# A fused decoder step: the first projected tile by feature blocks, a norm moved, a lane turn more, and sums of squares in two passes

## The chip, the cores and the metric

The kernel runs on one core of a Trainium2 chip. The core has a matrix engine (TensorE, PE in the profile; its weight loads are listed apart as PEld), a vector engine (DVE), a scalar engine (ACT), GpSimd (POOL) and a queue engine (SP) that issues most transfers. The metric is device microseconds of one execution, the median over the runs; lower is better.

## The reference, cut to what matters

Two layers of a hybrid decoder run on 512 prompt tokens and 32 sample tokens that share every weight. Inputs are scaled so that the attention weights are sharp, and all is float32. What the change touches:

```
hn = rmsnorm(x, norm_g);  z = hn @ w_in            # 10080 columns, 79 tiles of 128
k  = rmsnorm((rmsnorm(mem, g) @ w_k) by head, gk)  # memory keys, 256 rows
c  = rmsnorm(kv_lat, kv_norm_g)                    # kv_lat: 128 columns of z
qf = rmsnorm(q_lat, q_norm_g) @ w_uq               # q_lat: 192 columns of z
y_hg = rmsnorm(o_hg by head, hg_g)                 # after the HGRN recurrence
x  = x + merged @ w_out
```

`rmsnorm` divides a row by the root of the mean of its squares. The rest (short convolution, HGRN2 recurrence, attention over latents in pages and over memory keys, gated branch outputs) is in the kernel but is not edited.

## The kernel before

Everything is kept with features on the 128 partitions and the 544 tokens along the free axis, so a sum over features is a matrix product with a matrix of ones. A large product takes a weight block of 128 x 1024 at a time (an item): the scalar engine copies it to a type float32r (`wh`, the high part), the vector engine subtracts that from the float32 block (`wl`, the low part), and TensorE adds three products per feature block and half of the tokens (272 columns): high x high, high x low, low x high, in float32r. The activations are split the same way (`Hh`, `Hl` of the normed x). An item of `w_in` is 48 such products. A `wh`/`wl` pair of buffers exists twice, so the pair of the next item but one waits until an item has been multiplied.

The main loop goes over 254 items per execution: 8 of memory keys and values (`mk`, `mv`), then per layer the projected tiles C (the latent of keys), B and A (query latent and rope), `mq` (memory query), the others, and at the end 8 of `w_out`. Between the two halves of an item it takes a turn of lane `a` (memory attention, HGRN recurrence), after an item a turn of lane `b` (latent attention); a turn runs to the next `yield`. Items 30 to 99 of a layer give lane `b` no turn at every fourth item. The names `ta`, `tb` (`ra`, `rb` when float32r) are the lanes' buffers of 128 x 544, `sm` and `big` are accumulators, `sl` and `s` are two pools of six small tiles each. The framework puts the instructions of all engines in order by a built-in timeline, so an edit can shift instructions far from it; each engine then runs its own list strictly in that order.

What the prediction's steps touch, by name in the code: `xn_finish` (inverse norm of x, its broadcast by TensorE as `sm<-cst,sl`, then per block `e`, `Hh`, `Hl`); `ev_memk`, which sums the squares of the memory keys, normalizes and multiplies by the gain `kgb`, and `memk_T`, eight transposes of those keys at L514; `z_mm`, the products of an item; `rstd_big`, which turns sums into inverse roots by ACT (copy with epsilon, a table load, logarithm, a table load, exponential, square) and two DVE steps; and in `lane_b` the norm of C, then the norm of the query latent (tiles A and B), then `q_mm` for four heads, whose first product reads the normed `qA`. The sums of squares of C, of the query latent and of the four HGRN heads multiply by `ones`, a float32 matrix.

Of the kernel before, what the change touches and what calls it, by code (L numbers as in the profile page):

```python
# [19 lines left out]
P = 128  # L20
# [5 lines left out]
KD = 8  # L26
# [109 lines left out]
def hybrid_kernel(ctx: ExitStack, tc: tile.TileContext, a, o):  # L136
# [32 lines left out]
    def mm(out, lhsT, rhs, start=True, stop=True):  # L169
        return TE.matmul(out, lhsT, rhs, start=start, stop=stop)  # L170

    def act(out, in_, f, **k):
        S.activation(out, in_, f, **k)  # L173
# [54 lines left out]

    ident = cs_("id", P)
    ones = kp.tile([P, P], F32, name="ones")  # L230
    epsc = kp.tile([P, 1], F32, name="epsc")
    row4 = kp.tile([P, 4, P], F32R, name="row4")
    csq = kp.tile([P, T], F32, name="csq")

    def setup_first():
        V.memset(ones, 1.0)
        V.memset(epsc, EPS)
        x = t("b")[:, 0:4 * P].rearrange("p (h q) -> p h q", h=4)
        G.memset(x, 0.0)
        for h in range(4):  # L240
            G.memset(x[32 * h:32 * h + 1, h, :], 1.0)
        V.tensor_copy(row4, x)
        G.memset(cnew, 0.0)
        S.dma_start(out=gn, in_=a["gains"])
# [37 lines left out]
    def rstd_big(srcs, n, rows=P):  # L282

        v, y, z = t(), t(), t()
        w = 0
        for ap in srcs:
            k = ap.shape[-1]
            act(v[:rows, w:w + k], ap, AF.Identity, scale=1.0 / n, bias=epsc[:rows])
            w += k
        v, yv, z = v[:rows, :w], y[:rows, :w], z[:rows, :w]  # L290
        act(yv, v, AF.Ln)
        act(yv, yv, AF.Exp, scale=-0.5)
        act(z, yv, AF.Square)
        stt(z, z, -0.5, v, ALU.mult, ALU.mult)
        stt(yv, z, 1.5, yv, ALU.add, ALU.mult)
        return y

    def rstd_small(ss, n, alloc=None, eng=None):

        rows, w = ss.shape  # L300
        alloc = alloc or s_
        v, y, z = (x[:rows, :w] for x in (alloc(), alloc(), alloc()))
        ts(v, ss, 1.0 / n, EPS, ALU.mult, ALU.add)
        ts(y.bitcast(I32), v.bitcast(I32), -0.5, float(0x5F3759DF), ALU.mult, ALU.add)
        for _ in range(3):
            if eng is None:
                tt(z, y, y, ALU.mult)
                stt(z, z, -0.5, v, ALU.mult, ALU.mult)
                stt(y, z, 1.5, y, ALU.add, ALU.mult)
            else:  # L310
                tt(z, y, y, ALU.mult, eng=eng)
                tt(z, z, v, ALU.mult, eng=eng)
                ts(z, z, -0.5, 1.5, ALU.mult, ALU.add, eng=eng)
                tt(y, y, z, ALU.mult, eng=eng)
        return y
# [38 lines left out]
    def z_mm(l, key):  # L354
        def run(it, half):
            if half == 0:
                it.ps = big()
            Hh, Hl = st[l]["H"]
            for k in range(KD):
                w = slice(k * P, (k + 1) * P)  # L360
                c = slice(half * HT, (half + 1) * HT)
                for n, (x, y) in enumerate(((it.hi, Hh), (it.hi, Hl), (it.lo, Hh))):
                    mm(it.ps[:, half, 0:HT], x[:, w], y[:, k, c], start=(k == 0 and n == 0), stop=(k == KD - 1 and n == 2))
        return run

    def proj_mm(l):
# [41 lines left out]
    def ps2(it):  # L408
        return it.ps[:, :, 0:HT]
# [76 lines left out]

    def ev_memk(l):
        def run(it):
            ss = s_()
            kr = []  # L490
            for mt in range(2):
                x, q = t(), t("b")
                act(x[:, 0:512], it.ps[:, mt, :], AF.Copy, scale=rmem[:, mt:mt + 1])
                act(q[:, 0:512], it.ps[:, mt, :], AF.Square, scale=rmem[:, mt:mt + 1])
                red(ss[:, 4 * mt:4 * mt + 4], q[:, 0:512].rearrange("p (h d) -> p h d", h=4), ALU.add)
                kr.append(x)
            r = rstd_small(ss[:, 0:8], P)
            for mt in range(2):
                kv = kr[mt][:, 0:512].rearrange("p (h d) -> p h d", h=4)
                tt(kv, kv, bc(r[:, 4 * mt:4 * mt + 4], P), ALU.mult)  # L500
                tt(kv, kv, bcl(kgb[:, l, :], 4), ALU.mult)
                defer(2, lambda mt=mt: SY.dma_start(out=o["mk"][l, :, mt, :], in_=kr[mt][:, 0:512]))
            st[l]["kr"] = kr
        return run

    def memk_T(l):
# [23 lines left out]
    def ev_C(l):  # L530
        def run(it):
            lane[0] = "b"
            st[l]["kvr"], st[l]["sqkv"] = t(), t()
            act(v2(st[l]["kvr"]), ps2(it), AF.Copy)
            act(v2(st[l]["sqkv"]), ps2(it), AF.Square)
        return run

    def ev_B(l):
# [16 lines left out]
    def ev_A(l):  # L555
        def run(it):
            lane[0] = "b"
            qA, sqA = t(), t()
            act(v2(qA), ps2(it), AF.Copy)
            act(v2(sqA), ps2(it), AF.Square)  # L560
            st[l].update(qA=qA, sqA=sqA)
        return run

    def ev_mq(l, h):
# [272 lines left out]
    def hgrn(l, h):  # L837
# [190 lines left out]
        act(ob[:, 0:TP], ps, AF.Copy)  # L1028
        act(ob[:, TP:T], pso[:, 0:32], AF.Copy)
        act(sq, ob, AF.Square)  # L1030
        yield
        srcs = [sm(), sm()]
        for hf in range(2):
            mm(srcs[hf][:, 0:HT], ones, sq[:, hf * HT:(hf + 1) * HT])
        r = rstd_big([p[:, 0:HT] for p in srcs], P)
        stt(ob, ob, g_("hgn", 4 * l + h), r, ALU.mult, ALU.mult)
        st[l]["yh", h] = ob
        yield
# [2 lines left out]
    def lane_b(l):  # L1041
# [6 lines left out]
        SY.dma_start(out=wuqA[:, 0:512], in_=a["wuq"][l, 0:P])  # L1048
        G.memset(wuqB[64:128, 0:512], 0.0)
        SY.dma_start(out=wuqB[0:64, 0:512], in_=a["wuq"][l, P:192])  # L1050
        kvr, sqkv, qA, qB, sqA, sqB, rt, r2 = (st[l].pop(k) for k in ("kvr", "sqkv", "qA", "qB", "sqA", "sqB", "rt", "r2"))
        srcs = [sm(), sm()]
        for hf in range(2):
            mm(srcs[hf][:, 0:HT], ones, sqkv[:, hf * HT:(hf + 1) * HT])
        r = rstd_big([p[:, 0:HT] for p in srcs], P)
        cT = kvr
        stt(cT, kvr, g_("kv", l), r, ALU.mult, ALU.mult)
        defer(2, lambda: SY.dma_start(out=o["c"][l], in_=cT))
        yield
        srcs = [sm(), sm()]  # L1060
        for hf in range(2):
            c = slice(hf * HT, (hf + 1) * HT)
            mm(srcs[hf][:, 0:HT], ones, sqA[:, c], stop=False)
            mm(srcs[hf][:, 0:HT], ones, sqB[:, c], start=False)
        r = rstd_big([p[:, 0:HT] for p in srcs], 192)
        stt(qA, qA, g_("qa", l), r, ALU.mult, ALU.mult)
        stt(qB[0:64], qB[0:64], g_("qb", l, slice(0, 64)), r[0:64], ALU.mult, ALU.mult)
        ps = sm()
# [45 lines left out]
        def q_mm(h):  # L1114
# [11 lines left out]
                tt(tmp[64:96, c], ps[96:128, 0:HT], csq[96:128, c], ALU.mult)  # L1126
            tt(Q[64:96, h, :], Q[64:96, h, :], tmp[64:96, :], ALU.add)

        for h in range(4):
            q_mm(h)  # L1130
            yield
# [308 lines left out]

    def start_layer(l):
        def run():
            memk_T(l)
            lanes["a"] = lane_a(l)
            lanes["b"] = lane_b(l)
        return run
# [3 lines left out]
    for l in range(NL):  # L1450
        hg = [(w, h) for h in range(4) for w in ("hq", "hf", "hi")]

        def hg_items(h):
            for w in ("hq", "hf", "hi"):
                zi(l, (w, h), ev_h(l, w, h))

        zi(l, ("C",), ev_C(l), pre=start_layer(l))
        zi(l, ("B",), ev_B(l))
        zi(l, ("A",), ev_A(l))
        for h in range(4):  # L1460
            zi(l, ("mq", h), ev_mq(l, h))
        for i in range(4):
            zi(l, ("ch", i), ev_ch(l, i))
            zi(l, ("cc", i), ev_cc(l, i))
            zi(l, ("cb", i), ev_cb(l, i))
            zi(l, ("sg", CONV, i), ev_sg(l, CONV, i))

        def branch(n, before=None, after=None):
            for d in range(8):
                if before:  # L1470
                    before(d)
                zi(l, ("mg", n, d), ev_mg(l, n, d))
                add(l, ("pj", n, d), a["wb"][l, n, d], 512, proj_mm(l), ev_pj(l, n, d))

        branch(CONV, before=lambda d: hg_items(HG[0].index(d)) if d in HG[0] else None)
        for i in range(4):
            zi(l, ("sg", MEM, i), ev_sg(l, MEM, i), pre=drain(l, "a", "mem_done") if i == 0 else None)
        branch(MEM, before=lambda d: hg_items(len(HG[0]) + HG[1].index(d)) if d in HG[1] else None)
        for i in range(4):
            zi(l, ("sg", HGRN, i), ev_sg(l, HGRN, i), pre=drain(l, "a", "hg_done") if i == 0 else None)  # L1480
        branch(HGRN)
        for i in range(4):
            zi(l, ("sg", MLA, i), ev_sg(l, MLA, i), mm_=mla_mm(l, i), pre=drain(l, "b", "mla_done") if i == 0 else None)
        branch(MLA)
        for d in range(8):
            add(l, ("wo", d), a["wo"][l, d], 1024, out_mm(l), ev_out(l, d), pre=(lambda l=l: split_merged(l)) if d == 0 else None)
        if l + 1 < NL:
            mem_k(l + 1)
            mem_v(l + 1)
# [174 lines left out]
```

## Time and profile before

| | us |
|---|---|
| median of 3 runs | 1727.42 |
| lowest and highest of the runs | 1726.97, 1731.12 |
| the profiled execution, its own time | 1728.54 |
| its span, first to last instruction | 1726.0 |

The profile is one execution. A matrix product is listed with a modelled length that overlaps its neighbours, so the distance between starts says what it costs. A float32 product is listed as two records. A bracket at the end of a timeline row is the time in which the engine sat idle before it, and the engine and tile that ended it, as inferred from semaphores. In a row that ends in `x4`, four instructions were merged.

### The profile page before, as it was taken

The page shows a single profiled execution, that of the slowest core. Times are in us where ns is not written, and L with a number is a line of the kernel's source. Part 1 is how long each engine was busy: PE and PEld are TensorE (multiplying, and loading weights), DVE is VectorE, ACT ScalarE, POOL GpSimd, SP SyncE. Part 2 cuts the span into 40 slices and gives each one's busy share as a digit, 9 for nine tenths or more (in the row PEclk, how much of TensorE's full clock was granted, in tenths as well). Part 3 has the DMA queues.
Part 4 walks back from the last instruction along what each step waited for, and adds up shares of the span by engine and source line. Part 5 has one row for each costly group of instructions (what it writes and reads, how often), then busy time and mean ns, then how long its engine had stood idle before and what let it go on. Part 6 is the DMA issues. An engine that isn't in the chain of part 4 may idle for free.

```text
span 1726.0 us, 37508 instructions
## 1 busy us (share of the span) xinstructions
PE 1694.3 (98%) x14810; PEld 1626.0 (94%) x14810; DVE 1089.1 (63%) x2575; ACT 860.3 (50%) x1683; POOL 181.5 (11%) x258
## 2 busy tenths in 40 slices
PE   7999999999999999999999999999999999999999
PEld 6899899999989999999989989999999899999999
DVE  8575654678777876343574765556878788744343
ACT  6645444655757563222346554356666565622231
POOL 0010001112222220000000100011221231100000
PEclk9999999999999999999999999999999999999999
DMA  7212532344334443323553225323343434332233
GB/s 264 94 53 77 192 124 68 108 123 128 114 117 132 136 119 108 98 69 111 161 165 104 65 93 184 104 72 117 124 129 111 137 112 130 105 105 88 80 116 121
DMA packets 106834, 201.01 MB, mean 116 GB/s; under 512 B 13921, under 2 KB 48226, under 8 KB 106658
## 3 DMA queue, kind: packets, MB, share of 16 engines
q1 hardware_dynamic: 99346, 177.59, 32.7%
q0 software_dynamic: 7168, 20.98, 4.1%
q8 instruction: 116, 1.90, 0.5%
q14 instruction: 60, 0.49, 0.1%
q10 hardware_dynamic: 144, 0.04, 0.0%
HBM read 186.52 MB, written 12.04 MB: 115 GB/s over the span
## 4 chain that ended last, share of the span: by engine, by line
PE 86%; DVE 5%; ACT 4%; issue 2%; DMA 1%; SPq 1%; another core or an unknown queue 0%; ACTq 0%; DVEq 0%
PE big L170 66%; PE sm L170 18%; DVE wl L179 1%; ACT ta L173 1%; ACT L173 1%; DMA tb<-in_latT 1%; ACT wh L173 1%; ACT tb L173 1%; DVE e L176 1%; DVE ta L179 1%; DVE Hl L179 0%; SPq L1253 0%; PE sm L1212 0%; PE sm L990 0%; PE sm L1293 0%
## 5 line engine op out<-in xcount | busy, mean ns | idle before, releaser
L170 PE MATMUL big<-Hh,wh 128*128 128x272 f32 x2528 | 743.9, 294 | 0.7 <-ACT Hh L173 0.3
L170 PE MATMUL big<-Hh,wl 128*128 128x272 f32 x2528 | 736.6, 291 | 4.0 <-DVE wl L179 4.0
L170 PE MATMUL big<-Hl,wh 128*128 128x272 f32 x2528 | 733.4, 290 | 3.5 <-DVE Hl L179 3.3
L170 PEld LDWEIGHTS big<-Hh,wh 128*128 128x128 f32 x2528 | 477.1, 189 | 8.9 <-issue 5.3
L170 PEld LDWEIGHTS big<-Hl,wh 128*128 128x128 f32 x2528 | 477.5, 189 | 7.3 <-DVE Hl L179 4.4
L170 PEld LDWEIGHTS big<-Hh,wl 128*128 128x128 f32 x2528 | 476.8, 189 | 7.6 <-DVE wl L179 5.7
L173 ACT ACTIVATE wh<-wr 128x1024 fp32r<-128x1024 f32 (+1 forms) x246 | 232.8, 946 | 435.4 <-PE big L170 351.7
L179 DVE TENSOR_TENSOR wl<-wr,wh 128x1024 fp32r<-128x1024 f32 (+1 forms) x246 | 266.4, 1083 | 223.6 <-ACT wh L173 218.7
L173 ACT ACTIVATE tb<-sm 128x256 f32<-128x256 f32 (+6 forms) x380 | 141.0, 399 | 97.0 <-PE sm L170 73.0
L170 PE MATMUL big<-ysh,wh 128*128 128x272 f32 x512 | 148.8, 291 | 0.0
L170 PE MATMUL big<-ysh,wl 128*128 128x272 f32 x512 | 148.7, 290 | 0.0
L170 PE MATMUL big<-ysl,wh 128*128 128x272 f32 x512 | 148.1, 289 | 0.0
L173 ACT ACTIVATE ta<-ta 128x544 f32<-128x544 f32 (+3 forms) x180 | 96.0, 539 | 50.2 <-DVE ta L179 31.5
L179 DVE TENSOR_TENSOR ta<-ta 128x256 f32<-128x256 f32 (+3 forms) x251 | 111.0, 479 | 10.1 <-ACT ta L173 6.9
L170 PE MATMUL sm<-ta 128*32 128x32 f32 (+5 forms) x2192 | 107.1, 242 | 6.2 <-issue 5.8
L170 PE MATMUL sm<-Rh,rb 128*128 128x272 f32 x512 | 107.9, 298 | 2.0 <-DVE S L1285 1.2
L188 DVE TENSOR_REDUCE s<-tb 128x8 f32<-128x512 f32 (+1 forms) x150 | 100.4, 671 | 5.8 <-issue 4.3
L170 PEld LDWEIGHTS sm<-ta 128*32 128x32 f32 (+1 forms) x2192 | 82.3, 124 | 20.9 <-issue 12.2
L170 PEld LDWEIGHTS big<-ysl,wh 128*128 128x128 f32 x512 | 96.7, 189 | 0.2 <-issue 0.2
L170 PEld LDWEIGHTS big<-ysh,wh 128*128 128x128 f32 x512 | 96.5, 188 | 0.0
L170 PEld LDWEIGHTS big<-ysh,wl 128*128 128x128 f32 x512 | 96.3, 188 | 0.1
L1231 POOL DMA_INDIRECT tb<-in_rop,row4i x64 | 67.6, 1056 | 269.6 <-issue 90.6
(237 smaller groups left out, 2406.1 us busy)
## 6 DMA issues: line engine op xcount, KB each, us to landing
wr<-in_w_in SPq DMA_DIRECT2D x158, 512.0 KB
wr<-in_wb SPq DMA_DIRECT2D x64, 256.0 KB
tb<-in_latT SPq DMA_DIRECT2D x256, 64.0 KB
ta<-in_mkT SPq DMA_DIRECT2D x32, 256.0 KB
ta<-in_mv SPq DMA_DIRECT2D x32, 256.0 KB
wr<-in_wo SPq DMA_DIRECT2D x16, 512.0 KB
ta<-in_shg SPq DMA_DIRECT2D x16, 256.0 KB
out_hgs<-ta SPq DMA_DIRECT2D x16, 256.0 KB
```

The lines of the kernel that those rows point to most:

```text
L170: return TE.matmul(out, lhsT, rhs, start=start, stop=stop)
L173: S.activation(out, in_, f, **k)
L176: V.scalar_tensor_tensor(out=out, in0=in0, scalar=sc, in1=in1, op0=op0, op1=op1)
L179: (eng or V).tensor_tensor(out=out, in0=in0, in1=in1, op=op)
L188: V.tensor_reduce(out=out, in_=in_, op=op, axis=AX.X, **k)
L1231: G.indirect_dma_start(out=out, out_offset=None, in_=a[src], in_offset=bass.IndirectOffsetOnAxis(ap=idx, axis=0))
```

## The change

Six edits. (1) `z_mm` for tile C multiplies both halves of a feature block before it goes to the next block, all in the item's first half. (2) The three products of a block come in the order high x high, low weight x high, high weight x low, for all tiles of `w_in`. (3) `ev_memk` keeps the sums of squares in a tile of pool `sl`; inverse root, products and transposes move to a function `norm_memk` before the item `mq` 0, where they stood in `ev_memk` and before item C. (4) `lane_b` takes one turn more before `q_mm`. (5) `parts` splits a tile of squares into a float32r copy (ACT) and the rest (DVE), and `col_sums` multiplies both with a float32r matrix of ones, `onesr`: twelve places (C and query latent, and four HGRN heads, in two layers). (6) The squares of query tiles A and B are added by DVE first, so that they are summed as one tile.

```diff
+        V.tensor_copy(onesr, ones)
...
+    def parts(x):
+        h, lo = tr(), tr()
+        act(h, x, AF.Copy)
+        tt(lo, x, h.bitcast(F32), ALU.subtract)
+        return h, lo
+    def col_sums(x):
+        srcs = [sm(), sm()]
+        for hf in range(2):
+            c = slice(hf * HT, (hf + 1) * HT)
+            for n in range(2):
+                mm(srcs[hf][:, 0:HT], onesr, x[n][:, c], start=(n == 0), stop=(n == 1))
+        return [p[:, 0:HT] for p in srcs]
...
-            for k in range(KD):
+            if key == ("C",):
+                kh = [(k, hf) for k in range(KD) for hf in range(2)] if half == 0 else []
+            else:
+                kh = [(k, half) for k in range(KD)]
+            for k, hf in kh:
...
-                for n, (x, y) in enumerate(((it.hi, Hh), (it.hi, Hl), (it.lo, Hh))):
+                for n, (x, y) in enumerate(((it.hi, Hh), (it.lo, Hh), (it.hi, Hl))):
...
     def ev_memk(l):
-            ss = s_()
+            ss = sl_()
...
-            r = rstd_small(ss[:, 0:8], P)
+            st[l]["kr"], st[l]["ssk"] = kr, ss
+        return run
+    def norm_memk(l):
+        def run():
+            kr = st[l]["kr"]
+            r = rstd_small(st[l]["ssk"][:, 0:8], P)
             for mt in range(2):
                 kv = kr[mt][:, 0:512].rearrange("p (h d) -> p h d", h=4)
                 tt(kv, kv, bc(r[:, 4 * mt:4 * mt + 4], P), ALU.mult)
                 tt(kv, kv, bcl(kgb[:, l, :], 4), ALU.mult)
...
-            st[l]["kr"] = kr
+            memk_T(l)
...
     def ev_C(l):
+            st[l]["sqkv"] = parts(st[l]["sqkv"])
...
     def ev_A(l):
+            tt(sqA, sqA, st[l].pop("sqB"), ALU.add)
+            st[l].update(qA=qA, sqA=parts(sqA))
...
         act(sq, ob, AF.Square)
-        yield
-        srcs = [sm(), sm()]
-        for hf in range(2):
-            mm(srcs[hf][:, 0:HT], ones, sq[:, hf * HT:(hf + 1) * HT])
-        r = rstd_big([p[:, 0:HT] for p in srcs], P)
+        sq = parts(sq)
+        yield
+        r = rstd_big(col_sums(sq), P)
...
     def lane_b(l):
-            mm(srcs[hf][:, 0:HT], ones, sqA[:, c], stop=False)
-            mm(srcs[hf][:, 0:HT], ones, sqB[:, c], start=False)
-        r = rstd_big([p[:, 0:HT] for p in srcs], 192)
+        r = rstd_big(col_sums(sqA), 192)
...
+        yield
         for h in range(4):
             q_mm(h)
             yield
...
     def start_layer(l):
-            memk_T(l)
...
-            zi(l, ("mq", h), ev_mq(l, h))
+            zi(l, ("mq", h), ev_mq(l, h), pre=norm_memk(l) if h == 0 else None)
```

How the lists of three engines change is shown at three places. First the vector engine in layer 0, where the norm of x begins (`sl<-sm` is its first step, `s` and later `sl<-tb` belong to the norms of memory and its keys), before:

```order
L179 TENSOR_TENSOR wl<-raw,wh 128x1024
L185 TENSOR_SCALAR sl<-sm 128x5
L179 TENSOR_TENSOR s<-s 128x2
L185 TENSOR_SCALAR sl<-sl 128x5
L176 SCALAR_TENSOR_TENSOR s<-s 128x2
L179 TENSOR_TENSOR sl<-sl 128x5
```

and changed:

```order
L185 TENSOR_SCALAR tb<-tb,cst 128x32
L188 TENSOR_REDUCE sl<-tb 128x4
L185 TENSOR_SCALAR sl<-sm 128x5
L253 CAST row4i<-tb 128x32
L188 TENSOR_REDUCE sl<-tb 128x4
L185 TENSOR_SCALAR sl<-sl 128x5
L179 TENSOR_TENSOR wl<-raw,wh 128x1024
L185 TENSOR_SCALAR s<-sl 128x8
L179 TENSOR_TENSOR sl<-sl 128x5
```

The first step of the norm of x now stands behind the first reduction of the keys' squares, with which it shares a pool, and its later steps alternate with those of the keys' norm; before, it stood one weight split earlier and had the engine nearly to itself after that.

Second, TensorE where tile C begins in layer 0 (numbers tell tiles apart: big_520 and wh_480 are C before, big_488 and wh_462 are C now, the other pair is B), before:

```order
L170 MATMUL big_520<-Hh_414,wh_480 128x272
L170 MATMUL big_520<-Hl_415,wh_480 128x272
L170 MATMUL big_520<-Hh_414,wl_481 128x272
L170 MATMUL big_520<-Hh_414,wh_480 128x272
L170 MATMUL big_581<-Hh_414,wh_502 128x272
L170 MATMUL big_581<-Hl_415,wh_502 128x272
L170 MATMUL big_581<-Hh_414,wl_503 128x272
```

and changed:

```order
L170 MATMUL big_488<-Hh_396,wh_462 128x272
L170 MATMUL big_488<-Hh_396,wl_463 128x272
L170 MATMUL big_553<-Hh_396,wh_484 128x272
L170 MATMUL big_553<-Hh_396,wl_485 128x272
L170 MATMUL big_488<-Hl_397,wh_462 128x272
L170 MATMUL big_488<-Hh_396,wh_462 128x272
L170 MATMUL big_488<-Hh_396,wl_463 128x272
L170 MATMUL big_488<-Hl_397,wh_462 128x272
```

Per feature block there were 6 products that could run (half of C, half of B), now there are 9 (both halves of C, half of B): ahead of the first product with the last `Hl` stand 44 products before and 66 now. The eight transposes at L514 stood among these tiles, two of them ahead of that product; now all eight stand behind B. The broadcast `sm<-cst,sl` stood before the last 12 products of the memory values and now stands behind them; in layer 1 it stays where it was.

Third, the scalar engine at the query latent's norm in layer 0 (`tb<-sm,epsc` is its first step), before:

```order
L173 ACTIVATE ta<-big,mqg 128x544
L173 ACTIVATE ta<-big 128x544
L173 ACTIVATE tb<-sm,epsc 128x272 x2
L173 ACT_TABLE_LOAD
L173 ACTIVATE tb<-tb 128x544
L173 ACT_TABLE_LOAD
L173 ACTIVATE tb<-tb 128x544 x2
L173 ACTIVATE ctokP<-sm 128x512
```

and changed:

```order
L173 ACTIVATE ta<-big 128x544
L173 ACTIVATE wh<-wr 128x1024
L173 ACTIVATE tb<-tb 128x544
L173 ACTIVATE tb<-sm,epsc 128x272 x2
L173 ACT_TABLE_LOAD
L173 ACTIVATE tb<-tb 128x544
L173 ACT_TABLE_LOAD
L173 ACTIVATE tb<-tb 128x544 x2
L173 ACTIVATE ta<-big,mqg 128x544
```

A weight copy and the square of the norm of C (`tb<-tb`) now stand directly ahead of the query's norm. On TensorE the distance from the last sum of squares of the query to the first `q_mm` was 64 products of `w_in` and is 93; in both, five transposes stand between.

## Rows read from the trace of the kernel before

**Rows 1.** The page, parts 1 (engines) and 4 (chain that ended last).

```profile
PE 1694.3 (98%) x14810; PEld 1626.0 (94%) x14810; DVE 1089.1 (63%) x2575; ACT 860.3 (50%) x1683; POOL 181.5 (11%) x258
...
PE 86%; DVE 5%; ACT 4%; issue 2%; DMA 1%; SPq 1%; another core or an unknown queue 0%; ACTq 0%; DVEq 0%
```

**Rows 2.** Timeline, TensorE: start us, us, engine, line, operation, out<-in, count [idle before].

```profile
55.95 0.29 PE L170 MATMUL big<-Hl,wh 128*128 128x272 f32 x1
56.07 1.08 PE L170 MATMUL sm<-tb,ones 128*128 128x272 f32 x4
56.79 0.49 PE L170 MATMUL big<-Hh,wl 128*128 128x272 f32 x1
57.11 0.28 PE L170 MATMUL big<-Hh,wh 128*128 128x272 f32 x1
57.23 0.29 PE L170 MATMUL big<-Hl,wh 128*128 128x272 f32 x1
```

**Rows 3.** Tile `ones`: count, ns min/median/max, first to last start, forms.

```profile
L170 PE MATMUL sm<-tb,ones x72: 195/393/617, 56.1 to 993.0; 96*32 96x512 f32 x32, 128*128 128x272 f32 x24, 96*128 96x32 f32 x16
...
L170 PE MATMUL sm<-ta,ones x48: 391/393/617, 99.5 to 1469.0; 128*128 128x272 f32 x32, 128*32 128x512 f32 x16
```

**Rows 4.** Groups by line, vector then scalar engine: count, busy us, mean ns, idle before.

```profile
L179 DVE TENSOR_TENSOR Hl<-e,Hh 128x544 fp32r<-128x544 f32 x16 | 11.2, 715 | 0.0
...
L173 ACT ACTIVATE Hh<-e 128x544 fp32r<-128x544 f32 x16 | 10.5, 656 | 8.5 <-DVE e L176 8.1
```

**Rows 5.** Timeline, TensorE, the first query product of each layer.

```profile
80.82 1.16 PE L170 MATMUL sm<-tb 128*128 128x272 f32 x4 [1.43 <-ACT wh L173]
...
935.11 1.15 PE L170 MATMUL sm<-tb 128*128 128x272 f32 x4 [1.42 <-ACT wh L173]
```

**Rows 6.** Timeline, scalar engine, the norm of the query latent, layer 0.

```profile
72.88 0.86 ACT L173 ACTIVATE tb<-sm,epsc 128x272 f32<-128x272 f32 x2
...
77.03 1.35 ACT L173 ACTIVATE tb<-tb 128x544 f32<-128x544 f32 x2
```

**Rows 7.** Timeline, vector engine, end of the query norm, layer 0.

```profile
78.41 1.49 DVE L176 SCALAR_TENSOR_TENSOR tb<-tb 128x544 f32<-128x544 f32 x2 [4.14 <-ACT tb L173]
79.94 1.48 DVE L176 SCALAR_TENSOR_TENSOR tb<-tb,gn 128x544 f32<-128x544 f32 x2
```

**Rows 8.** Timeline, vector engine, the norm of x and its blocks, layer 0.

```profile
24.62 0.15 DVE L185 TENSOR_SCALAR sl<-sm 128x5 f32<-128x5 f32 x1
...
29.05 0.68 DVE L188 TENSOR_REDUCE s<-tb 128x4 f32<-128x512 f32 x1
...
47.78 0.71 DVE L179 TENSOR_TENSOR Hl<-e,Hh 128x544 fp32r<-128x544 f32 x1
```

**Rows 9.** Timeline, TensorE, broadcast and first projected tile, layer 0.

```profile
31.51 1.20 PE L170 MATMUL sm<-cst,sl 128*128 128x128 f32 x10
...
35.88 0.39 PE L170 MATMUL big<-Hh,wh 128*128 128x272 f32 x1 [0.31 <-ACT Hh L173]
...
40.30 0.43 PE L170 MATMUL big<-Hh,wl 128*128 128x272 f32 x1
...
47.30 0.39 PE L170 MATMUL big<-Hl,wh 128*128 128x272 f32 x1 [1.48 <-DVE Hl L179]
...
48.54 0.39 PE L170 MATMUL big<-Hl,wh 128*128 128x272 f32 x1
```

**Rows 10.** Windows: engines' busy us, clock; the half clock in layer 0, and its middle.

```profile
39.90:43.00 3.10, 3.09 (x13) 3.09 (x14) 3.10 (x7) 1.03 (x2) 0.00 (x0) 0.50 0.62 186
...
300.00:700.00 400.00, 393.21 (x3896) 384.46 (x3895) 299.78 (x758) 231.53 (x489) 73.93 (x92) 1.00 0.39 120
```

**Rows 11.** Timeline, TensorE, first projected tiles of layer 1.

```profile
896.46 0.40 PE L170 MATMUL big<-Hh,wl 128*128 128x272 f32 x1 [0.48 <-DVE wl L179]
...
899.58 0.39 PE L170 MATMUL big<-Hh,wl 128*128 128x272 f32 x1 [0.59 <-DVE wl L179]
```

**Rows 12.** Waits, TensorE for the low weights: us, times, longest.

```profile
PE big L170 <- DVE wl L179: 4.0, 8, 0.7
```

More of the change, by code (lines that the diff above doesn't have):

```diff
@@ L230, in hybrid_kernel @@
     ones = kp.tile([P, P], F32, name="ones")
+    onesr = kp.tile([P, P], F32R, name="onesr")
     epsc = kp.tile([P, 1], F32, name="epsc")
@@ L358, in run @@
             Hh, Hl = st[l]["H"]
-            for k in range(KD):
+            if key == ("C",):
[3 more added lines that the diff above has]
+            for k, hf in kh:
                 w = slice(k * P, (k + 1) * P)
-                c = slice(half * HT, (half + 1) * HT)
-                for n, (x, y) in enumerate(((it.hi, Hh), (it.hi, Hl), (it.lo, Hh))):
-                    mm(it.ps[:, half, 0:HT], x[:, w], y[:, k, c], start=(k == 0 and n == 0), stop=(k == KD - 1 and n == 2))
+                c = slice(hf * HT, (hf + 1) * HT)
+                for n, (x, y) in enumerate(((it.hi, Hh), (it.lo, Hh), (it.hi, Hl))):
+                    mm(it.ps[:, hf, 0:HT], x[:, w], y[:, k, c], start=(k == 0 and n == 0), stop=(k == KD - 1 and n == 2))
         return run
@@ L560, in run @@
             act(v2(sqA), ps2(it), AF.Square)
-            st[l].update(qA=qA, sqA=sqA)
+            tt(sqA, sqA, st[l].pop("sqB"), ALU.add)
+            st[l].update(qA=qA, sqA=parts(sqA))
         return run
@@ L1050, in lane_b @@
         SY.dma_start(out=wuqB[0:64, 0:512], in_=a["wuq"][l, P:192])
[L1051 to L1055, printed above, removed]
+        kvr, sqkv, qA, qB, sqA, rt, r2 = (st[l].pop(k) for k in ("kvr", "sqkv", "qA", "qB", "sqA", "rt", "r2"))
+        r = rstd_big(col_sums(sqkv), P)
         cT = kvr
@@ L1059, in lane_b @@
         yield
-        srcs = [sm(), sm()]
-        for hf in range(2):
-            c = slice(hf * HT, (hf + 1) * HT)
-            mm(srcs[hf][:, 0:HT], ones, sqA[:, c], stop=False)
-            mm(srcs[hf][:, 0:HT], ones, sqB[:, c], start=False)
-        r = rstd_big([p[:, 0:HT] for p in srcs], 192)
+        r = rstd_big(col_sums(sqA), 192)
         stt(qA, qA, g_("qa", l), r, ALU.mult, ALU.mult)
```

## The prediction, made before the changed kernel ran

> **What bounds the kernel now.** I read the page first: TensorE is busy 98% of the span and holds 86% of the chain that ended last [rows 1]. So an edit is worth what it takes out of TensorE's list or out of that engine's waits, and work on the vector and scalar engines costs nothing until TensorE waits for it. Then TensorE's timeline. The products of a stream start about 0.125 us apart although each is listed with 0.29 us, so I count distances between starts [rows 2]. Last the waits. Those that this change can touch are the first query product of each layer, 1.43 and 1.42 us [rows 5], the first projected tile of layer 0, where the blocks of the normed x come late [rows 8, 9], that of layer 1 [rows 11], and eight waits for the low weights, 4.0 us in all [rows 12].
>
> **Sums of squares.** Before, a float32 product of 272 columns is two records. Four records take 57.11 - 55.95 = 1.16 us from the product ahead to the second one behind, less two ordinary distances of 0.125: 0.91 us, or 0.455 per product [rows 2]. The tile of ones has 24 + 32 records of that shape [rows 3], so 28 products: 28 x 0.455 = 12.7 us of TensorE's time. The change puts 48 float32r products there (8 for C, 8 for the query, 32 for the heads), the same type and width as the stream: 48 x 0.125 = 6.0 us. Gain 6.7 us. At the least favourable they would not overlap and cost their listed 0.29 us, 13.9 us, a loss of 1.2; on the other side I see no row under 0.12, a gain of 6.9. I take 6.7, since the stream they stand in is of this very kind.
>
> The distance of 0.125 us is 300 cycles of 2.4 GHz for 272 columns [rows 2]. The Trainium skill (TensorE: Matmul & The Clock Gate, Back-to-back issue gap) gives columns / 2.4 GHz plus 2.5 ns for a warm product by itself, here 116 ns; by that the 48 would take 5.6 us and the gain be 7.2. The rows differ from it, and the sum goes by the rows.
>
> What it adds elsewhere: twelve splits, 656 ns on ACT and 715 ns on DVE each, and two additions of 715 ns [rows 4]: 7.9 us on ACT and 10.0 us on DVE. In the middle of layer 0 DVE is busy 300 of 400 us and ACT 232 [rows 10], so TensorE's stream covers them, except where a head's norm delays a weight split. TensorE is idle 400 - 393.2 = 6.8 us in those 400. Each of the eight heads puts about 1.3 us ahead of its own inverse root, beside a stream in which eight weight splits are late already [rows 12]. Between nothing and half a microsecond for each of the eight heads (4 us) I take 0.7.
>
> **The turn before the query product.** The query norm starts on ACT at 72.88, its exponential at 77.03, the DVE steps at 78.41 and 79.94, so `qA` is there at 79.94 + 0.74 = 80.7 and the product starts at 80.82, 1.43 us late [rows 5, 6, 7]. In the changed list 29 products more stand ahead of it, 3.6 us, and the sums there are about 1.1 us shorter, so TensorE comes to it some 2.5 us later than the 79.2 at which it was ready, near 81.8. The norm of C moves with it: it is summed a tile later and ACT does it directly ahead of the query's. Counting ACT from the end of tile A with the durations of these rows, the query norm starts about 0.7 us later than now and `qA` is there near 81.3. So 0.5 us of slack, and both waits go: 2.8 us. If the slack is short by 1 us the gain is 1.8; it cannot be over 2.85. Next late there is the weight split of `mq` 3, which stands behind the query's DVE steps: near 83.1 against its use near 83.6, also hidden.
>
> **The first projected tile, layer 0.** Here the change gives and takes. It takes: the norm of x begins on DVE at 24.62 now, and in the changed list behind the reduction that stands at 29.05 [rows 8], near 29.4. Its eleven steps alternate with the keys' norm and two weight splits and end near 34.8, against 31.5 when TensorE starts the broadcast [rows 9]. The values' products end at 35.88 - 0.31 = 35.6 now and, with the broadcast behind them, near 34.5, so TensorE idles, then broadcasts until 36. ACT has a weight copy and two evacuations ahead of the copies, DVE the keys' products ahead of the second block, and the first `Hh` product starts near 39.5 instead of 35.88 [rows 9]. With 0.65 to 0.78 us per DVE step the last `Hl` is there near 50.1, now at 47.78 + 0.65 = 48.4 [rows 8]. TensorE has mostly waited before it, and after such a stretch it now runs at a granted clock of 0.50 (1.2 GHz) from 39.9 to 43.0 [rows 10], products listed with 0.43 instead of 0.29 us [rows 9] and 3.1 / 13 = 0.24 apart; I expect the same length of it after the later start, about 14 products.
>
> It gives: 66 products instead of 44 stand ahead of the last `Hl`. The first `Hl` is there at 42.0 (three blocks from 38.0, the keys' gains 1.2, the subtraction 0.65), and from then 62 remain: 14 x 0.24 + 48 x 0.125 = 9.4, so 51.4; then 30 of tiles C and B and eight transposes, 3.75 + 1.0: 56.1. Now that product starts at 48.54 [rows 9], and 52 products (6.5) and six transposes (0.8) end at 55.8. So no gain, 0.3 us lost; between -2 (the norm of x as early as now) and +3 (TensorE cold for longer) I keep both ends. The moved norm itself costs DVE nothing more; its transposes stand behind B and their keys are ready by then.
>
> **Layer 1.** There the engines' lists keep the order of the norm of x, and B's first product comes 30 products later, so the wait of 0.59 us [rows 11] goes. **Order of the products.** The low weights are wanted one product sooner. Where they are late already, 0.125 us is added: 8 waits, less the one that goes, 0.9 us [rows 12]. Elsewhere the second product has slack. Between 0 and 1.0.
>
> **The sum.** From the profiled execution's 1728.5: -6.7 (sums) + 0.7 (splits) - 2.8 (query) + 0.3 (first tile, layer 0) - 0.6 (layer 1) + 0.9 (order) = -8.2, which gives 1720.3. The median of the runs lies 1.1 us under that execution, so 1719.2 by the median. I predict 1720.
>
> **The rivals.** (a) The middle takes it back. The sums' gain of the heads, 32 of 48 products, is 3.3 us, and the splits stand where weights are already late. If each head's norm makes one weight split late by the usual 0.5 us of [rows 12] (8 heads, 4.0 us), the time is 1724. For it: DVE 75% busy there; against: TensorE waits only 6.8 us of 400. (b) Layer 0 loses. If the later norm of x keeps TensorE cold and waiting, +3 us and a query norm short of its turn by 1 us per layer, +2, give 1725. For it: a norm that starts 4.8 us later; against: 22 more products ahead. (c) The other side: lane `b` runs one turn later for the rest of each layer, against items of different length, and the turns of its paged part, 32 per layer, meet other items than now. It decides from 0.2 us per turn: 64 x 0.2 = 12.8 us, 1733. At 0.25 us, half of a usual late split, it is 16 us and 1736, slower. For it: waits of just that size [rows 12]; against: only eight of them now in two layers, and long and short items mostly take turns, so that a shift by one is largely a swap. (d) The change doesn't do what it says: float32r with two products costs what one float32 product did, 0.455 for two, and only the query's merged sum (4 products of 8 gone) is a gain, 1.8 us: 1725.
>
> **How the numbers follow.** About 0.3% (5.2 us) is what a measurement of this kernel can tell from no change: faster is under 1722.2, slower over 1732.6. The forecast with its bounds, 1714 to 1722, has 0.65; (a) 0.14, (b) 0.11, (c) 0.05, (d) 0.05. Of the forecast a little reaches over 1722.2 and of (a) and (b) a little stays under it, which I let cancel, and part of (c) ends at no change: faster 0.66, same 0.29, slower 0.05. The likeliest alone has 1714 to 1722; the range takes in (a), (b) and (d): 1713 to 1727.
>
> **What would show it.** Right: sums of squares in blocks of four records, about 0.5 us longer than without; no bracket at the first query product of either layer; the first `Hh` product of layer 0 near 39.5 and tile B done near 55; half clock there of about 3 us; in layer 1 one wait for low weights of 0.6 instead of two. Wrong: a first `Hh` product at 36 (the norm of x not late), more than twelve waits for low weights, or TensorE idle over 10 us between 300 and 700.

## The result, and the profile after

The changed kernel takes 1757.1 us (median of four runs, 1756.65 to 1757.79) against 1729.18 of the kernel before in the same session: ratio 1.0171, interval 1.0146 to 1.0195, 28 us slower. The forecast was 1720 with a range of 1713 to 1727, faster.

The page of after, the two lines that answer to [rows 1]:

```profile
PE 1701.6 (97%) x14802; PEld 1633.7 (93%) x14802; DVE 1099.0 (63%) x2590; ACT 870.3 (50%) x1697; POOL 195.0 (11%) x258
...
PE 85%; ACT 6%; DVE 5%; issue 2%; DMA 1%; SPq 0%; ACTq 0%; DVEq 0%
```

The span grew from 1726.0 to 1756.0 us, TensorE's busy time by only 7.3. So 1756.0 - 1701.6 = 54.4 us without work stand against 31.7: 22.7 of the 30 us are idle time. The windows of after (columns as in [rows 10]; behind the first, the eight stretches in which the granted clock was 0.50, its lower level of 1.2 GHz) show the rest:

```profile
300.00:700.00 400.00, 382.43 (x3747) 372.22 (x3748) 295.13 (x750) 231.27 (x483) 84.07 (x94) 0.98 0.39 118
40.70:47.50 6.80, 5.51 (x24) 5.51 (x25) 6.80 (x12) 2.27 (x5) 0.00 (x0) 0.50 0.21 78
446.90:453.70 6.80, 5.77 (x25) 5.77 (x26) 6.56 (x19) 2.86 (x7) 0.56 (x1) 0.50 0.19 60
539.05:542.45 3.40, 3.40 (x17) 3.40 (x16) 2.47 (x6) 2.47 (x5) 0.00 (x0) 0.50 0.59 199
559.55:562.90 3.35, 3.35 (x15) 3.35 (x16) 2.51 (x8) 2.02 (x5) 0.00 (x0) 0.50 0.39 102
1313.90:1320.65 6.75, 5.37 (x23) 5.38 (x24) 6.20 (x18) 3.21 (x8) 0.55 (x1) 0.50 0.24 80
1382.15:1385.50 3.35, 3.35 (x17) 3.13 (x15) 1.83 (x4) 2.00 (x7) 0.00 (x0) 0.50 0.00 2
1409.45:1412.80 3.35, 3.13 (x14) 3.13 (x15) 2.04 (x6) 3.15 (x6) 0.00 (x0) 0.50 0.69 241
1703.00:1706.35 3.35, 3.35 (x17) 3.35 (x16) 3.35 (x5) 1.14 (x2) 0.00 (x0) 0.50 0.66 240
```

and the two such stretches of the kernel before:

```profile
39.70:43.05 3.35, 3.14 (x14) 3.14 (x15) 3.35 (x8) 1.22 (x3) 0.00 (x0) 0.50 0.63 195
490.25:493.60 3.35, 3.33 (x20) 3.26 (x20) 2.92 (x9) 2.29 (x5) 0.62 (x1) 0.50 0.07 20
```

In the middle of layer 0 TensorE is idle 17.6 of 400 us, where it was 6.8 [rows 10]. And it runs at the half clock in eight stretches, 37 us together, each behind waits or stops of which the longest was 1.1 to 3.3 us, where the kernel before had two, 7 us. At half clock the products of the stream start 0.23 us apart instead of 0.125. TensorE was busy for 33.2 us in the eight stretches and 6.5 in the two, so by an estimate from these numbers the 26.8 us more cost 26.8 x (1 - 0.125 / 0.23) = 12. Idle 22.7 + half clock 12 - sums 6.7 = 28 of the 30 us; where the other 2 lie stays open.

Who was waited for (TensorE; engine, tile and line waited for, us, times, longest), which answers to [rows 12]:

```profile
PE big L170 <- DVE ta L651: 11.4, 4, 3.3
PE big L170 <- DVE wl L179: 10.1, 15, 1.3
...
PE sm L170 <- DVE S L1306: 5.6, 6, 2.9
...
PE big L170 <- ACT Hh L173: 3.1, 1, 3.1
PE sm L1314 <- DVE S L1306: 2.5, 3, 1.0
```

The first line is new: `ta<-big` at L651 is the copy that empties the accumulator of a forget tile (`hf`), and until it has run TensorE has no accumulator for the next item. The place in layer 0, TensorE:

```profile
443.11 0.42 PE L170 MATMUL sm<-Rh,rb 128*128 128x272 f32 x2
443.36 0.29 PE L170 MATMUL sm<-Rl,rb 128*128 128x272 f32 x1
444.65 0.66 PE L1314 MATMUL sm<-cst,tb 128*128 128x128 f32 x4 [1.00 <-DVE S L1306]
447.93 0.59 PE L170 MATMUL big<-Hh,wh 128*128 128x272 f32 x1 [2.62 <-DVE ta L651]
```

the scalar engine, a head's norm (`ta`) between squares of paged products (`tb<-sm`):

```profile
441.27 0.88 ACT L173 ACTIVATE ta<-sm,epsc 128x272 f32<-128x272 f32 x2
442.17 1.28 ACT L173 ACT_TABLE_LOAD   x1
443.46 0.66 ACT L173 ACTIVATE ta<-ta 128x544 f32<-128x544 f32 x1
444.02 0.64 ACT L173 ACTIVATE tb<-sm 128x256 f32<-128x256 f32 x2
444.68 1.28 ACT L173 ACT_TABLE_LOAD   x1
445.97 0.66 ACT L173 ACTIVATE ta<-ta 128x544 f32<-128x544 f32 x1
```

and the vector engine, whose copy of paged scores waits for such a square, with the copy of `hf` behind it:

```profile
446.94 0.17 DVE L1306 COPY S<-sm 128x16 f32<-128x16 f32 x1 [0.88 <-ACT tb L173]
447.03 0.21 DVE L176 SCALAR_TENSOR_TENSOR s<-s 128x64 f32<-128x64 f32 x1
447.16 0.72 DVE L651 TENSOR_SCALAR ta<-big 128x544 f32<-128x544 f32 x1
```

Why TensorE had nothing else to do there is seen in its own list. The windows of the lanes' products alone (`sm`; TensorE's busy us and count, clock, DMA) over the first three memory gates of layer 0 (items of `w_in` that gate the memory branch) together, and over the `hf` item that comes three items later, before:

```profile
390.04:419.97 29.93, 12.62 (x202) 1.00 0.41 132
...
440.22:448.37 8.15, 2.31 (x14) 1.00 0.19 48
```

and after:

```profile
385.61:404.52 18.91, 1.30 (x9) 1.00 0.44 136
...
426.10:447.93 21.83, 11.57 (x103) 0.98 0.53 168
```

202 records of lane products stood among these three items, now 9, and `hf` has 103 instead of 14 and takes 21.83 us instead of 8.15. The lanes' work comes in clumps, and in a clump one engine waits for the other with few products of a weight item left to cover it. This place alone is not the loss: from the first gate to the end of `hf` after takes 62.3 us against 58.3, since the three gates take 11.0 us less and `hf` 13.7 more. The twenty items of `w_in` behind it, to 683.18 us before and 696.00 after, take 248.1 instead of 234.8, and layer 1 shows the same, 4.0 and 13.6 us more. So most of the loss comes later, in places like it, such as the two other waits for `ta`.

### The profile page after: what moved, and what is told of

It reads as the page before. It is cut to its first block, busy times and chain, and to the rows that moved or that the text cites. A ratio compares the mean times of both kernels' runs of the same rounds, so it can differ in the third digit from the quotient of the medians.

```text
span 1756.0 us, 37516 instructions
## 1 busy us (share of the span) xinstructions
PE 1701.6 (97%) x14802; PEld 1633.7 (93%) x14802; DVE 1099.0 (63%) x2590; ACT 870.3 (50%) x1697; POOL 195.0 (11%) x258
## 4 chain that ended last, share of the span: by engine, by line
PE 85%; ACT 6%; DVE 5%; issue 2%; DMA 1%; SPq 0%; ACTq 0%; DVEq 0%
PE big L170 68%; PE sm L170 15%; ACT ta L173 2%; ACT L173 2%; DVE wl L179 1%; ACT wh L173 1%; DVE ta L179 1%; DMA tb<-in_latT 1%; ACT tb L173 1%; PE sm L1020 0%; DVE e L176 0%; PE sm L1233 0%; DVE s L188 0%; PE sm L771 0%; SPq L1274 0%
## 5 line engine op out<-in xcount | busy, mean ns | idle before, releaser
L170 PE MATMUL big<-Hh,wh 128*128 128x272 f32 x2528 | 745.1, 295 | 15.5 <-DVE ta L651 11.4
L170 PEld LDWEIGHTS big<-Hh,wl 128*128 128x128 f32 x2528 | 481.9, 191 | 13.1 <-DVE wl L179 10.7
L173 ACT ACTIVATE e<-big 128x544 f32<-128x544 f32 x104 | 64.8, 623 | 219.3 <-PE big L170 218.7
L170 PE MATMUL sm<-ta 128*32 128x32 f32 (+5 forms) x2192 | 103.1, 242 | 5.7 <-issue 5.3
L1252 POOL DMA_INDIRECT tb<-in_lat,row4i x64 | 74.7, 1167 | 260.2 <-PE sm L170 134.5
L188 DVE TENSOR_REDUCE s<-tb 128x8 f32<-128x512 f32 (+2 forms) x146 | 97.9, 672 | 4.8 <-ACT tb L173 4.7
```

Source lines behind the costliest of these rows:

```text
L188: V.tensor_reduce(out=out, in_=in_, op=op, axis=AX.X, **k)
L1252: G.indirect_dma_start(out=out, out_offset=None, in_=a[src], in_offset=bass.IndirectOffsetOnAxis(ap=idx, axis=0))
```

## The experiments

Times differ between sessions: the kernel before took 1713 us in some and 1724 to 1729 in others, so each ratio is against the kernel before in the same session, with its interval. Five sessions of runs ran on five chips (e1 to e4, e5 to e8, e9 to e12, e13 to e16, e17 and e18), so chip and session can't be told apart. Ranges in us count from the kernel before at 1727 to 1729; they are compared here as ratios.

**The turn.** Without the turn (e1), the turn alone in the kernel before (e2), and the turn given back later, so that only the query's place keeps it (e5):

```diff
 e1, from the changed kernel         e2, to the kernel before
-        yield                       +        yield
         for h in range(4):                   for h in range(4):
 e5, from the changed kernel
         k_mm(0)
-        yield
         k_mm(1)
```

> The changed kernel without the extra turn of lane b before the query products; all else as changed. Theory T (the turn): one turn more shifts the whole latent lane against the memory and HGRN lane; the 33 us between the 1757 measured and the forecast of 1720 to 1724 are TensorE's waits (50.6 us idle instead of 27.9) and the half clock behind them (seven stretches more than before, 15 us), all between a head's norm and the paged turns beside it. Then the time comes to 1720 to 1727. Rival S (the splits): the splits of squares keep the scalar and vector engines from the weights, whatever the turn; then it stays above 1748. Rival P (order of the products): the low weights wanted one product sooner; also above 1748.

> The kernel before with one edit, the extra turn of lane b before the query products. Theory T: the turn alone costs what the change lost, 20 to 35 us: 1749 to 1764, with TensorE idle 45 us or more. Rivals S and P: the turn alone removes the query wait of 1.4 us per layer and costs nothing: 1724 to 1730.

> The changed kernel with the extra turn before the query products, but the two key products of lane b, which stood in two turns, now in one, so that from there on lane b stands where it stood before. All else as changed. Theory T in its sharp form (what costs is where lane b meets lane a in the paged part, not the turn at the query): the loss goes as it does without the turn, and the query waits (1.05 us in each layer without the turn) go too: 2 to 4 us under the kernel without the turn, ratio 0.998 to 1.002. Rival: the turn costs at the query itself, by buffers held longer; then the ratio stays above 1.012.

e1: 1.0032 (1.0019 to 1.0045), 1718.59 against 1712.97; most of the loss goes, but 1720 to 1727 meant 0.995 to 0.999, so e1 lies above its range. e2: 1.0164 (1.0147 to 1.0181), 28 us, in its range, with TensorE idle for 41.4 us, a little under the 45 expected. e5: 1.0069 (1.0051 to 1.0086). So the turn alone costs as much as the whole change, and it costs where lane `b` meets lane `a` later, not at the query: e5 keeps it there, has no wait at the query product, and loses the clumps (199 records in the three gates and 36 in `hf`, as in e1). But e5 missed its range too, so there is a second loss.

Is it being late, or the meeting? One turn fewer (e11: `k_mm(0)` and `k_mm(1)` in one turn of the kernel before) and two turns more (e12).

> The kernel before with the two key products of lane b in one turn, so that lane b runs one turn earlier from there on instead of one later. Theory T (the loss comes from which paged turn meets which step of an HGRN head, and the kernel before stands at a good meeting): this costs too, 8 to 35 us: 1.005 to 1.020, with waits behind the evacuations of the forget tile or between paged products. Rival (a later lane is what costs, since its last turns run out of items): one turn earlier costs nothing or gains, 0.996 to 1.002.

> The kernel before with two extra turns before the query products. Theory T: the cost is that of another meeting, so it need not be larger than with one turn; between 1.003 and 1.025. Rival (each turn later costs its 28 us): 1.03 or more.

e11: 1.0029 (1.0016 to 1.0042), a smaller cost than expected, and its interval reaches into the rival's range; e12: 1.0118 (1.009 to 1.0145), less than one turn, in its range. The cost does not grow with the turns. It goes along with the clumps, of which that place is a sign and not a measure: lane products in those three items and in `hf` are 191 and 19 in e11, 83 and 117 in e12, and in e2:

```profile
385.98:404.90 18.92, 0.98 (x7) 1.00 0.46 148
...
424.82:444.74 19.92, 10.53 (x99) 0.98 0.53 160
```

**The sums alone (e4)**, the kernel before with `parts` and `col_sums` at all twelve places.

> The kernel before with the sums of squares alone changed: splits and two float32r passes at all twelve places, and the query's squares added first. Theory T with the price of the forecast: 28 float32 products at 0.455 us go, 48 float32r products at 0.125 us come, 6.7 us less, with up to 4 us of late weights: 1722 to 1727. Rival S: the splits cost the change's loss, 1745 or more. Rival (d) of the forecast: two float32r products cost as much as a float32 one, 1726 to 1728.

0.9963 (0.9949 to 0.9977): 1706.28 against 1712.97, 6.7 us less. The price of the forecast holds and the splits cost next to nothing here.

**The order of the products.** e3 takes it back in the changed kernel, e6 puts it alone into the kernel before, e10 is e6 with the old order in the last merge gate only.

```diff
-for n, (x, y) in enumerate(((it.hi, Hh), (it.hi, Hl), (it.lo, Hh))):    # before, e3
+for n, (x, y) in enumerate(((it.hi, Hh), (it.lo, Hh), (it.hi, Hl))):    # changed, e6
```

> The changed kernel with the three products of a block in the order of before (high x high, high x low, low weight x high); all else as changed, with the turn. Theory T: the loss stays for the most part, 1742 to 1757. Rival P: it goes, 1720 to 1727. In either case the wait for the low weights at the first product of the output projection (1.35 us in each layer after, 0.13 before) should be gone, since with the new order the last product of the merge gate reads the low part of x, which frees the high part one product sooner and lets the copies of the merged sum pass the weight copy: worth 1 to 4 us.

> The kernel before with one edit, the order of the three products in the tiles of x (low weights second). By the two runs with and without it in the changed kernel (1.0171 and 1.0117) it costs some 9 us there. Theory: of this stands by itself 1 to 3 us per layer at the first output projection (1.35 us of wait and a half-clock stretch of 1.7 us), and 0.1 to 0.5 us at each late weight split: ratio 1.002 to 1.006. Rival: it costs only together with the turn, 0.999 to 1.001 here.

> The kernel before with the new order of products in all tiles of x but the last merge gate, which keeps the old one, so that its last product again reads the high part of x. Theory (the new order frees that buffer one product sooner, and copies of the merged sum pass the weight copy of the first output item): the waits of 1.35 us at that item and the half clock behind them go in both layers, 5 us of the 18 that the order costs by itself: ratio 1.006 to 1.009 where those stalls of the small HGRN products that had no wait for data come as before, 1.002 to 1.005 where they do not. Rival: the wait stays, 1.0105.

e3: 1.0117 (1.01 to 1.0134), in the range of theory T, and the wait at the first output item is gone in both layers, as expected. e6: 1.0105 (1.0089 to 1.012), 18 us and far over what was expected. e10: 1.0095 (1.0069 to 1.0121), just over its range. Two parts of the 18 can be seen. In e6 the first output item of a layer waits, at 829.80 us and again in layer 1:

```profile
827.94 0.40 PE L170 MATMUL big<-Mh,wh 128*128 128x272 f32 x1 [0.15 <-ACT wh L173]
829.80 0.39 PE L170 MATMUL big<-Mh,wl 128*128 128x272 f32 x1 [1.35 <-DVE wl L179]
```

With the half clock behind it that item takes 9.26 us, from its first product to that of the next item, in e6 and 6.76 in e10, in both layers: 5.0 us by the traces. The times alone don't tell the two kernels apart, since the intervals of 1.0105 and 1.0095 overlap. The cause is the one expected: the last product of the last merge gate no longer reads `Hh`, so the copies of the merged sum into that buffer pass the weight copy. The second part, 9.1 us, lies at the first memory gate of each layer (13.81 and 14.49 us instead of 9.58 and 9.59), in stalls of small products that are told below. The rest, some 4 us, fits the late weights, the term that the forecast had priced (waits for `wl` 9.4 us against 4.0, of which 2.7 at the output items), but was not shown apart.

So the loss of the changed kernel, 29 us of 1713 by its ratio, splits into the turn, 28.4 (e2), the four edits beside turn and order, -8.2 (e3 against e2, same session), and the order, the 9 that remain (1.0171 against 1.0117, two sessions). Alone in the kernel before the order cost 18 (e6), so these costs don't simply add.

**The first tile.** e8: the changed kernel without the turn and with the old order. e7: sums, tile C by blocks and the turn given back, but the keys' norm left in its place. e9: the changed kernel with the old order, the turn given back, and one line mended:

```diff
     def ev_memk(l):
-            ss = sl_()
+            ss = s_()
```

> The changed kernel without the turn and with the old order of products: what is left is sums, tile C by feature blocks and the keys' norm moved. Against the kernel before: sums 6.7 us less; the start of layer 0 by the trace of the kernel without the turn is 0.3 us better at the end of tile B, with the wait of 3.0 us for the first block and a half clock of 6.8 us that the kernel before does not have. So 1706 or 0.995 to 0.997. Rival: the moved norm costs the 3 us at the first block net: 0.997 to 0.999.

> The kernel before with the sums of squares in two passes, tile C by feature blocks with the old order of products, and the turn before the query products given back at the key products; the keys' norm where it was. Expected from the traces: sums 6.7 us (measured), the query waits of 2.85 us before (0.70 and 0.67 still there with the sums alone: 1.4 more to win), the waits of the first tile of layer 0 (3.8 us of idle and 1.7 of half clock) covered in part by 22 products more ahead of the last block, 0.6 in layer 1: ratio 0.991 to 0.994. Rival: the first tile gains nothing since its products then run out as early as the blocks come: 0.995 to 0.997.

> All six edits with three of them mended: the keys' sums of squares back in pool s while their norm still stands before mq 0, the old order of products, and the turn at the query given back at the key products. Theory (the shared pool made the norm of x late): the first product of tile C in layer 0 starts near 35.6 instead of 39.6, the first block's wait of 3.1 us goes, and the kernel comes within 3 us of the one that leaves the keys' norm where it was: ratio 0.991 to 0.994. Rival (the later place of the keys' norm itself makes the first tile late): 39 or later and 0.995 or more.

e8: 0.9963 (0.995 to 0.9977). e7: 0.9931 (0.9917 to 0.9944), 1718.27 against 1728.82. e9: 0.9945 (0.9925 to 0.9966), 1716.81 against 1726.12, just above its range. The first products of tile C in after and in e9:

```profile
39.45 0.39 PE L170 MATMUL big<-Hh,wh 128*128 128x272 f32 x1 [3.10 <-ACT Hh L173]
41.99 0.60 PE L170 MATMUL big<-Hl,wh 128*128 128x272 f32 x1 [1.77 <-DVE Hl L179]
```

```profile
35.94 0.31 PE L170 MATMUL big<-Hh,wh 128*128 128x272 f32 x1
37.27 0.39 PE L170 MATMUL big<-Hl,wh 128*128 128x272 f32 x1 [1.02 <-DVE Hl L179]
...
52.51 0.29 PE L170 MATMUL big<-Hh,wh 128*128 128x272 f32 x1
```

The shared pool alone made the norm of x late by 3.5 us: in e3 and e8, with the old order and with or without the turn, the first product still came at 39.74 and 39.62. With the pool mended the blocks' order gains: tile A, behind C and B, begins at 52.51 (the last line) instead of 55.82 before, and there is no half clock ahead of it. e7 and e9 are the same within their intervals, and both beat the kernel before by 9 to 11 us.

**What stops TensorE in a clump.** e13 (e2), e14 (the kernel before), e15 (the changed one) and e16 (e9) put the copy of the scores ahead of the square of the same accumulator:

```diff
+V.tensor_copy(g["S"][:, 4 * q + j, :], ps[:, 256:272])
 act(sq[:, j2 * 256:(j2 + 1) * 256], ps[:, 0:256], AF.Square)
-V.tensor_copy(g["S"][:, 4 * q + j, :], ps[:, 256:272])
```

> The kernel before with the extra turn, and in each paged product the vector engine's copy of the scores put ahead of the scalar engine's square of the same accumulator. Theory Q (the vector engine's list stands still at these copies, behind squares that wait for a head's table loads): the four waits of 13.0 us for the forget tile's evacuation fall to 6 or less, and with them half-clock stretches of 3.41 us; the kernel comes from 1.0164 to 1.004 to 1.011. Rival R (TensorE's own list is what stops it: a run of lane products with no product of a weight item between them, whatever the other engines' order): 1.014 or more.

> The kernel before with the copies ahead of the squares, without the turn: the control. Both theories: little, since the kernel before waits only 1.2 us for a score copy: 0.997 to 1.003.

> The changed kernel with the copies ahead of the squares. Theory Q: the waits for the forget tile's evacuation (11.4 us in four) fall to 5 or less, the waits for score copies (8.1 us in nine) to 3 or less, so 1.0171 comes to 1.004 to 1.012. Rival R: 1.015 or more.

> The kernel with all six edits, three of them mended (keys' sums in pool s, old order, the turn given back), with the copies ahead of the squares. It waits 3.3 us in four places for score copies: 0.991 to 0.995 against 0.9945 without, by theory Q 2 to 4 us better, by R the same.

e13: 1.0154 (1.0139 to 1.017). e14: 0.9994 (0.9985 to 1.0003). e15: 1.016 (1.0144 to 1.0175). e16: 1.0 (0.9991 to 1.0009), a miss: no better than the kernel before, though in another session than e9, with 8.1 us of new waits at L1352 for the scalar engine. The early gain is there all the same: against e14, measured beside it, the 31st item of `w_in` begins 5.3 us earlier (312.94 and 318.23), and by the 64th 0.8 is left (672.41 and 673.23). Theory Q falls. In e13 the waits only moved; its first lines, and those of e2:

```profile
PE sm L1294 <- ACT tb L173: 10.3, 4, 3.6
...
PE big L170 <- DVE ta L621: 5.9, 2, 2.9
```

```profile
PE big L170 <- DVE ta L621: 13.0, 4, 3.6
```

TensorE now waits for the squares themselves, which free its four accumulators `sm`. Are the table loads ahead of them the cause? e17 is e2 and e18 the kernel before with `AF.Copy` for `AF.Ln` and `AF.Exp` in the eight head norms; every engine's list is otherwise word for word the same.

> The kernel before with the extra turn; in the norms of the eight HGRN heads the logarithm and the exponential are replaced by plain copies of the same size, so the inverse roots of the heads are left out and their 16 table loads of 1.283 us with them; every other instruction stands where it stood with the turn. Theory S (the norm on the scalar engine stands ahead of the squares that free the four accumulators, 4.7 us of which 2.57 are table loads): the four waits of 13.0 us fall to about 3, most half-clock stretches behind them go, and of 1.0164 there remains 1.001 to 1.007. Rival R (TensorE's list alone): 1.013 or more.

> The kernel before with the same part left out, without the turn: the control. Both theories: the loads are covered there, 0.994 to 1.000.

e17: 1.0126 (1.0098 to 1.0153). e18: 0.9974 (0.9961 to 0.9988). The turn costs 1.0152 between the two, nearly as with the loads. The waits shrink (`ta` from 13.0 to 7.9 us) but stay, and the list is as clumped (7 and 99 lane products). So theory S falls too: e17 lies just under the range of R and far above that of S, and it stays above that of S if the 3.7 us by which its stops of small products (last section) exceed those of e18 are taken off. What is left is R, the clumped list, which leaves many small waits bare, whichever engine ends them. That the turn causes most of the loss is shown by e1, e2 and e5, and that clumps come along with it by their lists and those of e11 and e12. That the clumps are the cause is argued from the rivals that fell: no run kept the turn and spread the lanes' products evenly. Why the framework lists a head's products up to three items later when lane `b` runs one turn later stays open.

## Why the prediction was wrong

- **Rival (c), "long and short items mostly take turns, so that a shift by one is largely a swap"**, is the step that failed: by that reason the sum put the later turns of lane `b` at nothing. The mechanism was named, with 0.05, from 0.2 us per turn; the turn alone costs 28 us (e2), over twice that price, and not as half-late weights of each turn but in a few long waits, four of them at `ta` (13.0 us in e2, 11.4 in the changed kernel), with half clock behind. The order of the lists was compared only where a term of the sum stood, and not through the middle, where 202 lane products became 9.
- **"Order of the products ... 0.9 us"**: the term that was mis-sized by far, 18 us alone in the kernel before (e6) and 9 in the changed kernel (1.0171 to 1.0117). It priced the late weights that were there and missed that the order changes which tile the last product reads, and with it the lists; of the 18 us, 5.0 come from that (e6 against e10), 9.1 lie at the first memory gates, most of it in stops that the kernel before did not have there.
- **Sums, -6.7 + 0.7**: right, 6.7 us (e4). Two float32r products stand between their neighbours as two of the stream do, 63.27 to 63.52; answers to [rows 2].

```profile
63.15 0.29 PE L170 MATMUL big<-Hl,wh 128*128 128x272 f32 x1
63.27 0.41 PE L170 MATMUL sm<-rb,onesr 128*128 128x272 f32 x2
63.52 0.28 PE L170 MATMUL big<-Hh,wh 128*128 128x272 f32 x1
```

- **Query, -2.8**: right. (The rows give 80.82 - 1.43 = 79.4, not 79.2, for the time at which TensorE was ready before; nothing hangs on it.) `qA` was forecast for 81.3 and came at 81.85, TensorE at 82.66 without a wait (81.8 forecast), in both layers; answers to [rows 5].

```profile
82.66 1.08 PE L170 MATMUL sm<-tb 128*128 128x272 f32 x4
```

- **First tile, +0.3**: the first `Hh` product was forecast near 39.5 and came at 39.45, tile A begins 0.3 us later than before (56.10 against 55.82), as forecast. This is luck in part: the half clock lasted 6.8 us instead of 3.1 (24 products instead of 14, some 0.1 us more for each), and the eight transposes, priced at 1.0 us ahead of tile A, came behind its first product. Answers to [rows 8 to 10]. **Layer 1**: one wait of 0.60 instead of two, as forecast [rows 11].
- Rivals (a), (b) and (d): (a) is the nearest in place, but e4 shows that the splits are not its cause; (d) falls with e4; (b) was right that the norm of x comes late, and its 3 us net did not come.
- Two of the named signs of a wrong forecast came: over twelve waits for low weights (15) and over 10 us idle between 300 and 700 (17.6).

## What to carry to other kernels

Where a framework orders two interleaved lanes, a turn more or fewer moves every later meeting: compare the whole lists before and after, by lane products per weight item, and look for items with none and items with many. An edit that helps at one place can keep its gain if the turn is given back soon after (e5, e9). Before a tile changes pool or a product changes its place, ask who else takes from that pool and which buffer its last reader frees.

## What was not expected of the hardware

A block of 64 records of small products (32 columns of weights, 32 of the other operand), the same in both kernels, runs without a stop in one session, e1:

```profile
394.33 0.35 PE L170 MATMUL sm<-m,ones 128*128 128x16 f32 x2
394.61 0.76 PE L170 MATMUL sm<-ta 128*32 128x32 f32 x64
```

and stops five times in another, e5, with nothing waited for that the profile shows, and the half clock behind it:

```profile
393.81 0.55 PE L170 MATMUL sm<-ta 128*32 128x32 f32 x38
394.54 0.20 PE L170 MATMUL sm<-ta 128*32 128x32 f32 x1 [0.19 <-issue]
395.25 0.23 PE L170 MATMUL sm<-ta 128*32 128x32 f32 x2 [0.51 <-issue]
396.01 0.27 PE L170 MATMUL sm<-ta 128*32 128x32 f32 x4 [0.52 <-issue]
396.76 0.26 PE L170 MATMUL sm<-ta 128*32 128x32 f32 x3 [0.49 <-issue]
397.49 0.47 PE L170 MATMUL sm<-ta 128*32 128x32 f32 x16 [0.47 <-issue]
```

That item took 9.05 us in e1 and 13.74 in e5. In the sessions of e1 to e4 and e13 to e16, where the kernel before took 1713 us, these stops are 0 to 1.4 us in each kernel; in the others 0.7 to 9.4. Most of the second part of e6's cost is of this kind, so the order may cost less where they are missing: by the ratios of e8 and e1 it is 12 us, from two sessions. The gains of e7 and e9 were measured only where the stops occur. Whether the stops belong to the chip or to something else of the session is open, since each session had its own chip, and what ends them was not tried.
